# Fetching cached keys page by page through SyncE's queue, and scoring them with four full-height products per sequence

## The chip, the cores and the metric

The kernel runs on one NeuronCore of a Trainium2 chip. The metric is the device time of one execution in microseconds (us), lower being better. Engines are written as in the profile: PE is TensorE (PEld its weight loads), DVE VectorE, ACT ScalarE, POOL GpSimd, SP SyncE, which here issues transfers only. "SPq" is SP's sequencer.

## What is computed

One step of a hybrid decoder layer, for a prompt (512 tokens) and for a sample group (8 sequences of 4 new tokens, with 2048 cached tokens each, kept in pages of 128 tokens). The part that the change touches is the sample group's sparse attention: an indexer scores all cached tokens, the 256 best are chosen, and attention runs over those, here as a mask over all scores.

```python
def dsa_sample(q, k_new, v_new, qi, ki_new, wi, ck, cv, cki, page_table):
    ki_past = cki[page_table].reshape(DB, PAST_LEN, IDX_DIM)   # 16 pages a sequence
    sc = index_scores(qi, wi, ki_all)                          # relu(q.k), weighted sum of 8 heads
    _, idx = lax.top_k(sc, topk)                               # 256 of 2052
    k_sel = ck[phys, off]; v_sel = cv[phys, off]               # 2 kv heads of 64
    return sparse_attend(q, k_sel, v_sel, valid)               # softmax over the chosen
```

Around it stand the input projection (`w_in`), a gated MLP, the prompt's own sparse attention, the memory's key and value projection (`mem_wkv`), the output projection (`w_out`), memory attention (`mem_wq`, `mem_wo`) and, after that, an expert layer that takes most of the time and that the change doesn't touch.

## The kernel before

**The weight stream.** Every projection goes through `wtile` (L219): a tile of weights (128 x 1024, 512 KB) is loaded on SP's queue (L225) into one of two raw buffers, ACT rounds it to a high half (L213), DVE subtracts for the low half (L217), and PE makes 24 products of the three combinations (L249 to L251). Two raw buffers and two of each half mean that the load of a tile waits until the tile two before it has been split. In the order of the program: 19 tiles wA (`w_in`), the memory's normalised input (memT), 8 tiles wKV, then for the first half of the tokens, h0, 8 tiles wO and 4 wMQ, and then the second half, h1, with its own 8 wO.

**Side work.** Between products `tick` lets generators step: the masks' search (L695 on ACT, L692 on DVE), the gated MLP, the prompt's attention (`attend`, L845: softmax L860 to L867, values L880 to L890), and the sample side `samples` (L1251). That is `sample_scores` (index products L1359), `sample_select` (the 256th best score by bisection, 32 bits; one bit is the pass L1413 over 128 x 544 and seven small instructions on DVE, 1412 to 1424), `sample_keys` (key products) and, when both select and keys are done, `sample_attend` (`front` L1531: mask and softmax pieces, `turn`, `values` L1549: 16 products per sequence, L1553, and a copy that frees the buffer). A loop at L469 holds h1 back until `attend` and the sample side have ended, as the sample side's memory is reused there.

**Cached data before.** `index_rows` (L1310) stands behind each of the later weight loads: 4 pairs, so 8 pages of index keys per load on SP's queue, 128 in all (32 KB each, L1319: a register load of the page number, then a DMA with that register in its address). Keys and values come on POOL's queue: `fetch_kv` (L1261) issues four indirect gathers per sequence (L1276) into one of three buffers `kv` (`RING`), and a buffer is fetched anew when its sequence has been used. Two of these three buffers first hold the index keys of sequences 4 to 7. Key scores take 64 products per sequence, each a quarter of the array (64 x 64) by 128 columns (L1496), with weights spread by DVE (`q4`, L1488), and two copies out on ACT (L1500).

Of the kernel before, what the change touches and what calls it, by code (L numbers as in the profile page):

```python
# [18 lines left out]
P = 128  # L19
NP = 512  # L20
NS = 32
# [30 lines left out]
class Kernel:  # L52
# [166 lines left out]
    def wtile(self, pool, src, kt=KT, n=P):  # L219

        more = pool is self.pw and self.gp is not None and self.RX
        if more:
            self.raws = (self.raws + 1) % (2 + self.RX)
        raw = self.t(self.gp, [P, kt, n], tag="wraw", bufs=self.RX) if more and self.raws > 1 else self.t(pool, [P, kt, n], tag="wraw", bufs=2)
        load = self.nc.sync.dma_start(raw, src)  # L225
        self.loads += 1
        if self.todo and self.loads > 2:
            self.index_rows(load)
        hi = self.t(pool, [P, kt, n], F32R, tag="whi", bufs=2)
        lo = self.t(pool, [P, kt, n], F32R, tag="wlo", bufs=2)  # L230
        self.split(hi, lo, raw)
        return hi, lo
# [1046 lines left out]
    def pages(self, s1, s2):  # L1279
        nc, I = self.nc, self.I  # L1280

        pid = self.t(s1, [P, 1])
        for r in range(0, P, 32):
            nc.gpsimd.iota(pid[r : r + 32], [[0, 1]], base=0, channel_multiplier=1, allow_small_or_imprecise_dtypes=True)
        pt_i = self.t(s1, [P, P], I32)
# [3 lines left out]
        self.s_ix = self.t(s1, [P, 64], I32)  # L1289
        tmp = self.t(s1, [P, 64])  # L1290
        for u in range(4):
            r = slice(u * 32, u * 32 + 32)

            nc.vector.tensor_scalar(tmp[r, :32].rearrange("p (b c f) -> p b c f", c=2, f=2),
                                    pf[r].rearrange("p (b c v r f) -> p v r b c f", c=2, v=2, r=2, f=2)[:, u % 2, u // 2],
                                    32.0, pid[r], ALU.mult, ALU.add)
            nc.vector.tensor_scalar(tmp[r, 32:], pf[r].rearrange("p (n u) -> p u n", u=4)[:, u], 32.0, pid[r], ALU.mult, ALU.add)
# [12 lines left out]
    def index_rows(self, behind):  # L1310
        nc = self.nc
        src = self.I["cI"].rearrange("(n d) x -> n d x", d=64)
        with self.tc.issue_after(getattr(behind, "ins", behind)):
            for pt_i, b, m in self.todo[: self.PAGES]:
                for c in range(2):
                    n = b * 16 + 2 * m + c
                    page = nc.values_load(pt_i[:1, n : n + 1], engines=[mybir.EngineType.SP], min_val=0, max_val=src.shape[0] - 1,
                                          skip_runtime_bounds_check_because="a page table holds pages of the pool")
                    nc.sync.dma_start(self.rows[b][c * 64 : c * 64 + 64, m, :], src[bass.ds(page, 1)].rearrange("n d x -> (n d) x"))  # L1319
        self.todo = self.todo[self.PAGES :]  # L1320

    PAGES = 4


    def sample_scores(self, s1, s2):
        nc, I = self.nc, self.I
# [4 lines left out]
        for c in range(2):  # L1331
            src = slice(c * 64, c * 64 + 64)
# [124 lines left out]
    def sample_keys(self, s1, s2):  # L1457
        nc = self.nc
# [9 lines left out]
        self.s_room = Room(qs.rearrange("p e b q -> p (e b q)"))  # L1468
        ps = self.pst("pb")
        for e in range(4):  # L1470
            perm = self.t(s1, [P, P], tag="qst", bufs=2)
            nc.vector.tensor_copy(perm.rearrange("p (u g d) -> p u g d", u=4, g=2),
                                  self.ident.rearrange("p (g e d) -> p e g d", g=2, e=4)[:, e].unsqueeze(1).to_broadcast([P, 4, 2, 16]))
            nc.tensor.matmul(ps[:, e * P : e * P + P], perm, self.s_q.rearrange("p r t -> p (r t)"), start=True, stop=True)
        for e in range(4):
            nc.scalar.activation(qs[:, e].rearrange("p b (r t) -> p r b t", r=4), ps[:, e * P : e * P + P].rearrange("p (r b t) -> p r b t", r=4, b=8),
                                 AF.Copy, scale=0.125)

        own = self.t(s2, [P, 4])
        nc.vector.tensor_reduce(own, self.ident.rearrange("p (r c d) -> p c r d", r=2, d=16), AX.XY, ALU.add)  # L1480
        yield 1.0
        while not self.indexed:
            yield 1.0
        S = [self.t(s1, [P, 4, 512], tag="S8", bufs=2) for _ in range(2)]
        self.s_S = [S[b // 4][:, b % 4, :] for b in range(8)]
        for b in range(8):
            q4 = self.t(s2, [P, 4, 64], tag="q4", bufs=2)
            nc.vector.tensor_tensor(q4.rearrange("p e (c q) -> p e c q", c=4), qs[:, :, b].unsqueeze(2).to_broadcast([P, 4, 4, 16]),  # L1488
                                    own.unsqueeze(1).unsqueeze(3).to_broadcast([P, 4, 4, 16]), ALU.mult)

            pair = [self.pst("pb") for _ in range(2)]
            for e in range(4):
                for f in range(2):
                    for o, ps in zip((0, 64), pair):
                        for c in range(2):
                            nc.tensor.matmul(ps[c * 64 : c * 64 + 64, f * P : f * P + P], q4[o : o + 64, e],  # L1496
                                             self.kv[b][o : o + 64, 2 * c + f, e * P : e * P + P], start=e == 0 and f == 0, stop=e == 3,
                                             skip_group_check=True, tile_position=(o, c * 64))
            for r, ps in enumerate(pair):
                nc.scalar.copy(self.s_S[b].rearrange("p (m r f x) -> p r f m x", m=4, r=2, f=2)[:, r],  # L1500
                               ps[:, : 2 * P].rearrange("p (f m x) -> p f m x", f=2, m=4))
            self.fetch_kv(s2)
            yield 4.0 * self.SK
        self.keyed = True

    SK = 1.0

    def sample_attend(self, s2, s1):
# [40 lines left out]
        def values(b, A):  # L1549
            po = self.pst("pb")  # L1550
            for m in range(4):
                for c in range(4):
                    nc.tensor.matmul(po[c * NS : c * NS + NS, :P], A[:, m, c, :], self.kv[8 + b][:, c, m * P : m * P + P],  # L1553
                                     start=m == 0, stop=m == 3)
            nc.scalar.copy(part(b), po[:, :P])
            self.fetch_kv(s2)
# [314 lines left out]
```

## Time and profile before

| what | value |
|---|---|
| runs shown | 1797.67 us median of 3, 1795.82 to 1801.38 |
| the profiled execution | 1793.41 us, span 1791.7 us |
| mean granted TensorE clock | 0.963 of full speed |
| busy share of the span | PE 94%, DVE 83%, ACT 48%, POOL 28% |
| stage up to the first h1 product | 0 to 403 us |

The span is the time from the first to the last instruction; the execution's own time has 1.7 us beside it. The profiled execution is 4.3 us under the median. A row of a timeline has its start, its length, the engine, the line, what it writes and reads; "[x <-Y]" is the engine's idle time before it and what ended that. A line of the windows has the busy time of each engine in a stretch and the granted clock as a share of full speed.

### The profile page before, as it was taken

What the parts mean: (1) busy time and instruction counts of PE and PEld (TensorE: products, weight loads), DVE (VectorE), ACT (ScalarE), POOL (GpSimd) and SP (SyncE); (2) the same over time, 40 slices, a digit from 0 to 9 for tenths busy, and PEclk for the clock granted to TensorE, in tenths of its full rate; (3) what the DMA queues carried; (4) which work ended last, traced back from release to release, by engine and by line L of the source; (5) the groups of instructions that cost most, each with busy time, mean ns of one, the idle gap of its engine ahead of it and who ended that gap; (6) DMA issues with size and microseconds to landing.
All of it is one profiled execution on the core that took longest, in us unless ns stands there. A gap on an engine that the chain in (4) does not pass through costs nothing. (4 is left out here: it accounts for less than half of the span.)

```text
span 1791.7 us, 30106 instructions
## 1 busy us (share of the span) xinstructions
PE 1675.7 (94%) x10494; PEld 1476.6 (82%) x10494; DVE 1482.9 (83%) x3654; ACT 863.2 (48%) x1584; POOL 503.6 (28%) x437
## 2 busy tenths in 40 slices
PE   7999889989996999799999999999999999999995
PEld 5879757778875889789899998888788888888884
DVE  4586899755759999998999887799898888878897
ACT  4355765764543434674675575233343333333333
POOL 3000123120000054223224222334333534345343
PEclk9999769989998999999999999999999999999997
DMA  5423425445752599789779789799998999999986
GB/s 179 128 83 98 126 85 199 140 166 170 238 172 90 169 345 329 267 316 334 256 269 322 242 306 316 267 353 333 360 356 300 375 357 328 349 334 324 358 305 231
DMA packets 195207, 460.36 MB, mean 257 GB/s; under 512 B 17976, under 2 KB 98616, under 8 KB 193648
## 3 DMA queue, kind: packets, MB, share of 16 engines
q1 hardware_dynamic: 132928, 241.63, 39.7%
q0 software_dynamic: 53072, 207.71, 32.5%
q10 hardware_dynamic: 9056, 9.11, 1.6%
q8 instruction: 82, 1.34, 0.3%
q14 instruction: 69, 0.57, 0.1%
HBM read 416.11 MB, written 42.05 MB: 256 GB/s over the span
## 5 line engine op out<-in xcount | busy, mean ns | idle before, releaser
L251 PE MATMUL t<-t,t 128*128 128x384 f32 (+3 forms) x2544 | 867.9, 346 | 12.5 <-DVE t L217 12.2
L250 PE MATMUL t<-t,t 128*128 128x384 f32 (+3 forms) x2544 | 867.6, 343 | 0.0
L249 PE MATMUL t<-t,t 128*128 128x384 f32 (+3 forms) x2544 | 779.9, 346 | 17.6 <-ACT t L213 15.1
L213 ACT CAST t<-t 128x1024 fp32r<-128x1024 f32 (+4 forms) x512 | 418.2, 841 | 716.8 <-PE t L250 475.8
L217 DVE TENSOR_TENSOR t<-t,t 128x1024 fp32r<-128x1024 f32 (+4 forms) x512 | 488.6, 965 | 140.0 <-ACT t L213 136.3
L251 PEld LDWEIGHTS t<-t,t 128*128 128x128 f32 x2544 | 485.0, 191 | 66.4 <-DVE t L217 15.7
L249 PEld LDWEIGHTS t<-t,t 128*128 128x128 f32 x2544 | 485.0, 191 | 61.2 <-ACT t L213 20.3
L250 PEld LDWEIGHTS t<-t,t 128*128 128x128 f32 x2544 | 485.4, 191 | 38.4 <-issue 5.7
L1276 POOL DMA_INDIRECT t<-in_u,t x160 | 201.7, 1260 | 499.0 <-DVE t L1736 305.0
L1276 POOL DMA_INDIRECT t<-in_v,t x160 | 215.5, 1347 | 298.0 <-DVE t L1741 233.9
L1741 DVE SCALAR_TENSOR_TENSOR t<-t,t,t 128x1024 f32<-128x1024 f32 x160 | 204.9, 1281 | 4.5 <-DMA t<-in_v,t 3.6
L1736 DVE SCALAR_TENSOR_TENSOR t<-t,t 128x1024 f32<-128x1024 f32 x160 | 193.8, 1219 | 8.7 <-DMA t<-in_u,t 8.6
L1081 ACT ACTIVATE t<-t 128x512 f32<-128x512 f32 x96 | 96.6, 1148 | 19.3 <-DMA wd<-t 18.5
L1276 POOL DMA_INDIRECT t<-in_cK,t x32 | 32.3, 1009 | 212.1 <-PE t L1359 146.5
L1217 DVE TENSOR_TENSOR t<-t,t 128x352 f32<-128x352 f32 x128 | 66.6, 521 | 6.2 <-DMA t<-wd 4.0
L1097 ACT ACTIVATE t<-t 128x384 f32<-128x384 f32 x128 | 62.3, 487 | 11.8 <-PE t L251 9.2
L1071 ACT ACTIVATE t<-t,t 128x128 f16<-128x128 f16 x192 | 58.2, 395 | 10.1 <-DVE t L1067 7.4
L1078 PE MATMUL t<-t,t 128*128 128x128 f16 x384 | 51.8, 221 | 9.4 <-ACT t L1081 8.8
L1276 POOL DMA_INDIRECT t<-in_cV,t x32 | 34.2, 1069 | 72.0 <-PE t L1553 45.1
L695 ACT ACTIVATE t<-t,t 128x384 f32<-128x384 f32 x64 | 42.7, 666 | 24.4 <-DVE t L692 20.3
L1079 PE MATMUL t<-t,t 128*128 128x128 f16 x384 | 49.7, 221 | 0.4 <-DVE t L1073 0.3
L1079 PEld LDWEIGHTS <-t 128*128 128x128 f16 x384 | 36.7, 98 | 10.6 <-issue 10.1
(400 smaller groups left out, 1471.2 us busy)
## 6 DMA issues: line engine op xcount, KB each, us to landing
t<-in_uT SPq DMA_DIRECT2D x128, 512.0 KB, 5.8
t<-in_v SPq DMA_DIRECT2D x128, 512.0 KB, 6.2
wd<-t POOLq DMA_DIRECT2D x11, 2048.0 KB, 9.2
t<-wd SPq DMA_DIRECT2D x32, 704.0 KB, 7.9
gd<-t SPq DMA_DIRECT2D x56, 192.0 KB, 5.3
t<-gd SPq DMA_DIRECT2D x56, 192.0 KB, 7.6
t<-in_wA SPq DMA_DIRECT2D x19, 512.0 KB, 4.0
t<-in_wO SPq DMA_DIRECT2D x16, 512.0 KB, 4.0
```

The lines of the kernel that those rows point to most:

```text
L213: self.nc.scalar.copy(hi, x)
L217: self.pin_v = self.nc.vector.tensor_tensor(lo, x, hi, ALU.subtract)
L249: mm(out, ah, bh, start=first, stop=False)
L250: mm(out, ah, bl, start=False, stop=False)
L251: self.pin = mm(out, al, bh, start=False, stop=last)
L1079: nc.tensor.matmul(o, oj[:, x, :], ol[:, x, :], start=False, stop=True)
L1081: nc.scalar.activation(wb[:, :, t : t + 4].rearrange("p i t -> p t i"), ps.rearrange("p (t i) -> p t i", t=4), AF.Copy, scale=1.0 / 2048.0)
L1097: nc.scalar.activation(G, ps, AF.Gelu_apprx_tanh)
L1217: nc.vector.tensor_tensor(q(w)[:, : 4 * NB - 1], self.wp[:, :, i % 4, :], q(G)[:, : 4 * NB - 1], ALU.mult)
L1276: self.nc.gpsimd.indirect_dma_start(out=out, out_offset=None, in_=src, in_offset=bass.IndirectOffsetOnAxis(ap=ix, axis=0))
L1736: nc.vector.scalar_tensor_tensor(r, r, 1.0, hf, ALU.mult, ALU.mult, accum_out=a[:, k : k + 1])
L1741: nc.vector.scalar_tensor_tensor(acc, r, a[:, k : k + 1], acc, ALU.mult, ALU.add)
```

## The change

Index pages and key pages form one list, `todo`, of (target, source, place in the page table). Behind every weight load after the second, `fetch_pages` issues the next 6 of it on SP's queue: first the 128 index pages, then 128 key pages (64 KB each, 128 x 128). Key pages of a sequence enter the list when its buffer is taken. `sample_keys`, before it scores a sequence, calls `fetch_pages` until that sequence's 16 pages have been issued, with a pause worth 4 us of ticks between the calls. Values are gathered as before. Key scores become four products per sequence, 128 x 32 by 512 columns, side by side in one PSUM bank, with one copy out. Lines below L1260 shift: page load L1281, index product L1357, key product L1485, copy L1487, a bit's pass L1411, `front`'s first softmax piece L1524, value products L1540, the last products of the sample side L1621 and L1622 (before L1634, L1635).

```diff
@@ wtile
-        load = self.nc.sync.dma_start(raw, src)
+        self.pin_s = self.nc.sync.dma_start(raw, src)
         self.loads += 1
-        if self.todo and self.loads > 2:
-            self.index_rows(load)
+        if self.loads > 2:
+            self.fetch_pages()
@@ fetch_kv
             kv = self.t(s2, [P, 2048], tag="kv", bufs=self.RING)
-            kv = kv.rearrange("p (m x) -> p m x", m=4)
-            for m in range(4):
-                self.gather(kv[:, m, :], self.I["cV" if n >= 8 else "cK"], self.s_ix[:, n * 4 + m : n * 4 + m + 1])
+            if n < 8:
+                src = self.I["cK"].rearrange("(n d) (e x) -> n e d x", d=32, e=4)
+                self.todo += [(kv[:, m * P : m * P + P], src, 16 * n + m) for m in range(16)]
+            else:
+                for m in range(4):
+                    self.gather(kv[:, m * 512 : m * 512 + 512], self.I["cV"], self.s_ix[:, (n - 8) * 4 + m : (n - 8) * 4 + m + 1])
...
+    def fetch_pages(self):
+        nc = self.nc
+        with self.tc.issue_after(getattr(self.pin_s, "ins", self.pin_s)):
+            for out, src, n in self.todo[: self.PAGES]:
+                page = nc.values_load(self.s_pt[:1, n : n + 1], engines=[mybir.EngineType.SP], min_val=0, max_val=src.shape[0] - 1,
...
+                x = src[bass.ds(page, 1)]
+                nc.sync.dma_start(out, x.rearrange("n d x -> (n d) x") if len(x.shape) == 3 else x[0])
+        self.todo = self.todo[self.PAGES :]
+
+    PAGES = 6
@@ pages (index_rows, with PAGES = 4 pairs, is gone; the gathers' indices shrink from 64 to 32 columns)
-        self.todo, self.loads = [(pt_i, b, m) for b in range(8) for m in range(8)], 0
+        src = I["cI"].rearrange("(n d) x -> n d x", d=64)
+        self.todo, self.loads = [(self.rows[b][c * 64 : c * 64 + 64, m, :], src, 16 * b + 2 * m + c) for b in range(8) for m in range(8) for c in range(2)], 0
@@ sample_scores
-            while any(x[1] == b for x in self.todo):
+            while len(self.todo) > 16 * (7 - b + len(self.kv)):
                 yield 1.0
@@ sample_keys
-        qs = self.t(s2, [P, 4, 8, 16])
...
+        perm = self.t(s1, [P, P], tag="qst", bufs=2)
+        nc.vector.tensor_copy(perm.rearrange("p (e g d) -> p e g d", e=4, g=2), self.ident.rearrange("p (g e d) -> p e g d", g=2, e=4))
         ps = self.pst("pb")
...
+        nc.tensor.matmul(ps[:, :256], perm, qb.rearrange("p b g r t -> p (b g r t)"), start=True, stop=True)
+        room = self.t(s2, [P, 512])
+        q3 = room[:, :256].rearrange("p (b q) -> p b q", b=8)
+        nc.scalar.copy(room[:, :256], ps[:, :256])
...
         for b in range(8):
-            q4 = self.t(s2, [P, 4, 64], tag="q4", bufs=2)
...
-            pair = [self.pst("pb") for _ in range(2)]
-            for e in range(4):
-                for f in range(2):
-                    for o, ps in zip((0, 64), pair):
-                        for c in range(2):
-                            nc.tensor.matmul(ps[c * 64 : c * 64 + 64, f * P : f * P + P], q4[o : o + 64, e],
...
-            for r, ps in enumerate(pair):
-                nc.scalar.copy(self.s_S[b].rearrange("p (m r f x) -> p r f m x", m=4, r=2, f=2)[:, r],
...
+            while len(self.todo) > 16 * (min(len(self.kv), 8) - b - 1):
+                self.fetch_pages()
+                yield self.SP
+            ps = self.pst("pb")
+            for c in range(4):
+                nc.tensor.matmul(ps[c * NS : c * NS + NS, :], q3[:, b], self.kv[b][:, c * 512 : c * 512 + 512],
+                                 start=True, stop=True)
+            nc.scalar.copy(self.s_S[b].rearrange("p (m u x) -> p u m x", m=4, u=4), ps.rearrange("p (u m x) -> p u m x", u=4, m=4))
             self.fetch_kv(s2)
             yield 4.0 * self.SK
         self.keyed = True
 
+    SP = 4.0
     SK = 1.0
```

**Where the order moves.** SP, from the fourth-last wKV tile on (t_3695 is its load; `in_wKV` and `in_wO` are weights, `in_cK` key pages; a page is a register load, an address step "ISA" and the DMA). Before:

```order
L225 DMA t_3695<-in_wKV 128x1024
L225 DMA t_3788<-in_wKV 128x1024
L225 DMA t_3878<-in_wKV 128x1024
L225 DMA t_3971<-in_wKV 128x1024
L225 DMA t_4083<-in_wO 128x1024
```

The same queue in the changed kernel, from the last wKV load (t_3472) to the first wO load (t_3656):

```order
L225 DMA t_3472<-in_wKV 128x1024
L1278 TENSOR_LOAD t_123
L1281 ISA
L1281 DMA t_2383<-in_cK 128x1x128
...
L1278 TENSOR_LOAD t_123
L1281 ISA
L1281 DMA t_2383<-in_cK 128x1x128
L225 DMA t_3656<-in_wO 128x1024
```

Ten pages now stand between these two loads. From behind the fifth wKV load to the fourth wMQ load of h0 there are 126 pages (2 of index keys, 124 of keys) and 15 loads; before there was none there.

PE, at the end of h0's last wMQ tile. Before, the products of that tile (t_5032, L249 to L251) alternate with the sample side's softmax (L1535) and values (L1553):

```order
L1553 MATMUL t_4748<-t_4474,t_4733 32x128 x16
L249 MATMUL t_5032<-t_152,t_5028 128x256
...
L1545 MATMUL t_4772<-t_60,t_2890 128x128 x4
L1535 LDWEIGHTS t_4779
L1535 MATMUL t_4778<-t_2676,t_4779 128x512
L250 MATMUL t_5032<-t_153,t_5028 128x256
...
L251 MATMUL t_5032<-t_152,t_5029 128x256
L778 MATMUL t_5114<-t_150,t_4870 128x256 x2
L1553 MATMUL t_4786<-t_4593,t_4771 32x128 x16
```

In the changed kernel the tile (t_4928) ends first, then the last key product stands (L1485), and behind it all of `sample_attend`, from the first softmax product (L1522) to the eighth value product, with h1's first product (t_5487) after it:

```order
L251 MATMUL t_4928<-t_144,t_4925 128x256
L1485 MATMUL t_4953<-t_4344,t_2598 32x512
...
L1522 LDWEIGHTS t_5004
L1522 MATMUL t_5003<-t_3527,t_5004 128x512
...
L1540 MATMUL t_5050<-t_4604,t_5015 32x128 x16
...
L1540 MATMUL t_5363<-t_5285,t_5356 32x128 x13
...
L1622 MATMUL t_5419<-t_2598,t_762 128x32 x4
L249 MATMUL t_5487<-t_5439,t_5483 128x288
```

Before, four of the eight value products (L1553) stand among projections; now none does.

DVE, around the split of the last wMQ tile (t_4906 is the raw tile; L1411 is a bit's pass) and the first of h1's wO tiles (t_5481):

```order
L1411 SCALAR_TENSOR_TENSOR t_3531,t_3548<-t_3530,t_3546,t_58 128x544
L1412 STREAM_TRANSPOSE t_3549<-t_3548 128x32
L1413 TENSOR_REDUCE t_3550<-t_3549 128x8
L217 TENSOR_TENSOR t_4925<-t_4906,t_4924 128x1024
...
L1411 SCALAR_TENSOR_TENSOR t_3531,t_3548<-t_3530,t_3546,t_58 128x544
...
L217 TENSOR_TENSOR t_5484<-t_5481,t_5483 128x1024
```

26 of the 32 bits stand in the changed order before the last wMQ split and 6 behind it; before the change all 32 stand before the split of the third wO tile.

## Rows read from the trace of the kernel before

**Rows 1.** Windows: us, busy of PE, PEld, DVE, ACT, POOL, then PEclk, DMA share, GB/s

```profile
210.00:251.00 41.00, 26.51 (x223) 18.61 (x222) 33.48 (x200) 31.20 (x96) 11.73 (x12) 0.54 0.27 78
251.00:308.00 57.00, 54.02 (x605) 44.32 (x605) 54.24 (x224) 32.35 (x77) 20.25 (x20) 0.97 0.50 162
...
371.00:403.00 32.00, 26.13 (x236) 20.41 (x235) 17.94 (x72) 17.82 (x54) 6.78 (x7) 0.84 0.45 157
```

**Rows 2.** PE timeline: start us, us, engine line op [idle before <-releaser]

```profile
221.07 5.45 PE L1496 MATMUL t<-t,t 64*64 64x128 f32 x64 [5.96 <-ACT t L1500]
...
251.19 0.58 PE L249 MATMUL t<-t,t 128*128 128x256 f32 x1
```

**Rows 3.** PE groups: count | busy us, mean ns | idle before

```profile
L1496 PE MATMUL t<-t,t 64*64 64x128 f32 x512 | 27.3, 322 | 9.6 <-ACT t L1500 9.6
...
L1672 PE MATMUL t<-t,t 128*32 128x256 f32 x64 | 4.5, 387 | 0.0
```

**Rows 4.** SP timeline, DMA issues: start us, us, what, how many

```profile
42.98 0.53 SPq L225 DMA_DIRECT2D t<-in_wA  x1
44.02 7.35 SPq L1319 DMA_DIRECT2D t<-in_cI  x8
...
144.51 24.20 SPq L1319 DMA_DIRECT2D t<-in_cI  x24
...
258.17 25.32 SPq L225 DMA_DIRECT2D t<-in_wKV  x4
...
333.03 15.49 SPq L225 DMA_DIRECT2D t<-in_wMQ  x4
```

**Rows 5.** One line's instructions on SP, L225: duration ns min/median/max

```profile
L225 SPq DMA_DIRECT2D t<-in_wKV x8: 327/328/382, 178.7 to 283.2; - x8
```

**Rows 6.** DMA issues: KB each, median us from issue to landing

```profile
t<-in_wA SPq DMA_DIRECT2D x19, 512.0 KB, 4.0
...
t<-in_cI SPq DMA_DIRECT2D x128, 32.0 KB, 2.0
```

**Rows 7.** ACT groups from 208 to 252

```profile
L695 ACT ACTIVATE t<-t,t 128x512 f32<-128x512 f32 (+1 forms) x25 | 16.7, 667 | 7.0 <-DVE t L692 6.8
L695 ACT ACTIVATION_READ_ACCUMULATOR t<-t,t 128x1 f32 x25 | 4.7, 187 | 0.0
```

**Rows 8.** ACT timeline: last squares of the memory, and the third wKV tile's split

```profile
207.88 0.42 ACT L132 ACTIVATE t<-t 128x256 f32<-128x256 f32 x1 [0.34 <-PE t L135]
...
255.75 1.05 ACT L213 CAST t<-t 128x1024 fp32r<-128x1024 f32 x1 [1.78 <-PE t L250]
```

**Rows 9.** DVE timeline: three bits' passes, then the first softmax piece of the attention

```profile
305.62 0.79 DVE L1413 SCALAR_TENSOR_TENSOR t<-t,t,t 128x544 f32<-128x544 f32 x1
...
307.98 0.79 DVE L1413 SCALAR_TENSOR_TENSOR t<-t,t,t 128x544 f32<-128x544 f32 x1
...
312.46 0.78 DVE L1413 SCALAR_TENSOR_TENSOR t<-t,t,t 128x544 f32<-128x544 f32 x1
...
333.70 0.69 DVE L1537 CUSTOM_DVE_ANT_0 t<-t,t 128x512 f32<-128x512 f32 x1
```

**Rows 10.** DVE groups of the page: the split of a weight tile

```profile
L217 DVE TENSOR_TENSOR t<-t,t 128x1024 fp32r<-128x1024 f32 (+4 forms) x512 | 488.6, 965 | 140.0 <-ACT t L213 136.3
```

**Rows 11.** PE timeline: last wMQ product, values of sequences 4 and 7, first h1 product

```profile
370.79 0.28 PE L251 MATMUL t<-t,t 128*128 128x256 f32 x1
...
371.86 1.08 PE L1553 MATMUL t<-t,t 128*32 128x128 f32 x32
...
384.39 1.08 PE L1553 MATMUL t<-t,t 128*32 128x128 f32 x32 [0.73 <-ACT t L1546]
...
403.10 0.48 PE L249 MATMUL t<-t,t 128*128 128x288 f32 x1
```

**Rows 12.** POOL timeline: gathers of one sequence's values

```profile
374.92 0.95 POOL L1276 DMA_INDIRECT t<-in_cV,t  x1 [0.30 <-PE t L880]
376.17 0.95 POOL L1276 DMA_INDIRECT t<-in_cV,t  x1 [0.30 <-issue]
```

More of the change, by code (lines that the diff above doesn't have):

```diff
@@ L1264, in fetch_kv @@
             kv = self.t(s2, [P, 2048], tag="kv", bufs=self.RING)
-            kv = kv.rearrange("p (m x) -> p m x", m=4)
-            for m in range(4):
-                self.gather(kv[:, m, :], self.I["cV" if n >= 8 else "cK"], self.s_ix[:, n * 4 + m : n * 4 + m + 1])
-            self.kv.append(kv)
+            if n < 8:
[4 more added lines that the diff above has]
+                    self.gather(kv[:, m * 512 : m * 512 + 512], self.I["cV"], self.s_ix[:, (n - 8) * 4 + m : (n - 8) * 4 + m + 1])
+            self.kv.append(kv)
+    def fetch_pages(self):
[3 more added lines that the diff above has]
+                page = nc.values_load(self.s_pt[:1, n : n + 1], engines=[mybir.EngineType.SP], min_val=0, max_val=src.shape[0] - 1,
+                                      skip_runtime_bounds_check_because="a page table holds pages of the pool")
+                x = src[bass.ds(page, 1)]
+                nc.sync.dma_start(out, x.rearrange("n d x -> (n d) x") if len(x.shape) == 3 else x[0])
+        self.todo = self.todo[self.PAGES :]
+    PAGES = 6
     RING = 3
@@ L1284, in pages @@
             nc.gpsimd.iota(pid[r : r + 32], [[0, 1]], base=0, channel_multiplier=1, allow_small_or_imprecise_dtypes=True)
-        pt_i = self.t(s1, [P, P], I32)
+        pt_i = self.s_pt = self.t(s1, [P, P], I32)
         nc.gpsimd.dma_start(pt_i, I["page_table"].rearrange("b n -> (b n)").partition_broadcast(P))
@@ L1288, in pages @@
         nc.vector.tensor_copy(pf, pt_i)
-        self.s_ix = self.t(s1, [P, 64], I32)
-        tmp = self.t(s1, [P, 64])
+        self.s_ix = self.t(s1, [P, 32], I32)
+        tmp = self.t(s1, [P, 32])
         for u in range(4):
             r = slice(u * 32, u * 32 + 32)
[L1294 to L1297, printed above, removed]
+            nc.vector.tensor_scalar(tmp[r], pf[r].rearrange("p (n u) -> p u n", u=4)[:, u], 32.0, pid[r], ALU.mult, ALU.add)
         nc.vector.tensor_copy(self.s_ix, tmp)
@@ L1304, in pages @@
             self.rows.append(kx[:, b % 2 * 2 : b % 2 * 2 + 2, :].rearrange("p b (m x) -> p (b m) x", x=P))
-        self.todo, self.loads = [(pt_i, b, m) for b in range(8) for m in range(8)], 0
+        src = I["cI"].rearrange("(n d) x -> n d x", d=64)
+        self.todo, self.loads = [(self.rows[b][c * 64 : c * 64 + 64, m, :], src, 16 * b + 2 * m + c) for b in range(8) for m in range(8) for c in range(2)], 0
         for _ in range(self.RING - 2):
             self.fetch_kv(s2)
[L1310 to L1314, printed above, removed]
-                for c in range(2):
[L1316 to L1322, printed above, removed]
     def sample_scores(self, s1, s2):
@@ L1465, in sample_keys @@
                 nc.vector.tensor_scalar(qb[r, :, g, q], self.s_q[r, q].rearrange("p (b t) -> p b t", t=4), 0.125, None, ALU.mult)
-        qs = self.t(s2, [P, 4, 8, 16])
-        self.s_room = Room(qs.rearrange("p e b q -> p (e b q)"))
+        perm = self.t(s1, [P, P], tag="qst", bufs=2)
+        nc.vector.tensor_copy(perm.rearrange("p (e g d) -> p e g d", e=4, g=2), self.ident.rearrange("p (g e d) -> p e g d", g=2, e=4))
         ps = self.pst("pb")
-        for e in range(4):
[L1471 to L1480, printed above, removed]
+        nc.tensor.matmul(ps[:, :256], perm, qb.rearrange("p b g r t -> p (b g r t)"), start=True, stop=True)
+        room = self.t(s2, [P, 512])
+        q3 = room[:, :256].rearrange("p (b q) -> p b q", b=8)
+        nc.scalar.copy(room[:, :256], ps[:, :256])
+        self.s_room = Room(room)
         yield 1.0
@@ L1486, in sample_keys @@
         for b in range(8):
-            q4 = self.t(s2, [P, 4, 64], tag="q4", bufs=2)
-            nc.vector.tensor_tensor(q4.rearrange("p e (c q) -> p e c q", c=4), qs[:, :, b].unsqueeze(2).to_broadcast([P, 4, 4, 16]),
-                                    own.unsqueeze(1).unsqueeze(3).to_broadcast([P, 4, 4, 16]), ALU.mult)
-            pair = [self.pst("pb") for _ in range(2)]
-            for e in range(4):
-                for f in range(2):
-                    for o, ps in zip((0, 64), pair):
-                        for c in range(2):
-                            nc.tensor.matmul(ps[c * 64 : c * 64 + 64, f * P : f * P + P], q4[o : o + 64, e],
-                                             self.kv[b][o : o + 64, 2 * c + f, e * P : e * P + P], start=e == 0 and f == 0, stop=e == 3,
-                                             skip_group_check=True, tile_position=(o, c * 64))
-            for r, ps in enumerate(pair):
-                nc.scalar.copy(self.s_S[b].rearrange("p (m r f x) -> p r f m x", m=4, r=2, f=2)[:, r],
-                               ps[:, : 2 * P].rearrange("p (f m x) -> p f m x", f=2, m=4))
+            while len(self.todo) > 16 * (min(len(self.kv), 8) - b - 1):
[6 more added lines that the diff above has]
+            nc.scalar.copy(self.s_S[b].rearrange("p (m u x) -> p u m x", m=4, u=4), ps.rearrange("p (u m x) -> p u m x", u=4, m=4))
             self.fetch_kv(s2)
```

2 lines of the change are left out of this document (1 added, 1 removed).

## The prediction, made before the changed kernel had run

> **What bounds the kernel now.** I read the page first: PE is busy 94% of the span, so only a stretch where PE idles or runs at its lower clock has something to give, and any stretch left bare of projections costs in full. Then the windows up to h1's first product, where the two programs differ; behind it they are the same but for small reorderings, so whatever that product shifts by, the end shifts by. Two stretches stand out. From 210 to 251 PE is busy 26.51 of 41.00 us at a granted clock of 0.54, and from 371 to 403 it is busy 26.13 of 32.00 at 0.84; between, from 251 to 308, it is busy 54.02 of 57.00 at 0.97 [rows 1]. A granted clock near 0.5 is the 1.2 GHz level, near 1 the 2.4 GHz level. The PE timeline shows the first stretch to be the block of key products, which wait up to 5.96 us for the ACT copies; the first wKV product comes at 251.19 [rows 2]. In the second stretch the projections have run out: the last wMQ product starts at 370.79, values of four sequences follow, and h1's first product starts at 403.10, when the sample side has ended [rows 11]. So the end is set by when the sample side ends: select on DVE, softmax, values. The SP view tells what paces the weights: in the wKV, wO and wMQ stages SP issues weight loads alone, held back by buffers, not by its own work [rows 4].
>
> **What the change removes.** 512 quarter products cost 27.3 us of PE and 9.6 us of idle before them. Four side by side with 256 columns cost 4.5 us for 64 products, so 0.28 us for four; at 512 columns I take double, 0.56, times 8 sequences: 4.5 us [rows 3]. With the 9.6 us gone too, the gain on PE would be 27.3 + 9.6 - 4.5 = 32 us if nothing else bound. The copies and spread queries that go on ACT and DVE lie beside other work; the 32 gathers of keys leave POOL, which isn't waited for there; both cost and give nothing by themselves.
>
> **Where that moves the start of wKV.** Two things. First, 24 index pages in one go held SP for 24.20 us behind the 17th wA load [rows 4]; with 6 pages behind each load the 18th goes out 18 x 0.95 = 17 us earlier. PE could use some of that only, as it was working on two loaded tiles; I take 8 us (bounds 0 and 17), so the memory's last squares come at 200 instead of 207.88 [rows 8]. Second, from those squares to the third wKV tile's split ACT took 47.9 us [rows 8]. In the changed order it has 9 passes of the masks' search there instead of 25; 16 fewer, at (16.7 + 4.7 + 7.0) / 25 = 1.14 us with their waits [rows 7], is 18 us, and six copies and the waits for the key block are another 3 to 6. That leaves 26: the split at 226, and the load behind it, which came 2.4 us after the split (258.17 against 255.75) [rows 4, 8], at about 229. First wKV product at about 222. At this point the changed kernel is 29 us ahead. I count it as 220 to 242 for the load of the fifth wKV tile.
>
> **What it adds: SP's queue.** From that load to the load of h0's fourth wMQ tile, SP issues 126 pages and 15 weight loads in the program's order, where before it issued weight loads alone. A page costs SP 7.35 / 8 = 0.92 us in a run behind a load and 24.20 / 24 = 1.01 in the long run; a load to the page behind it is 44.02 - 42.98 = 1.04 [rows 4]. I take 0.95: 126 x 0.95 + 15 x 1.04 = 135 us. The key pages are 64 KB where the rows are of 32 KB; a weight load of 512 KB costs SP 0.33 us [rows 5], so bytes are not what SP pays for; the register in the address is. So the load of the last wMQ tile goes out at 229 + 135 = 364, against at most 348.5 before (333.03 + 15.49) [rows 4]. Landing takes 4.0 us [rows 6], the two splits 2 to 3 on ACT and DVE, 0.97 of it DVE's [rows 10]: split at about 371. While SP paces, loads are 7 to 12 us apart and PE, with 3 us of products a tile, waits on each; the 29 us of lead are gone.
>
> Here the Trainium skill ("DMA: Bandwidth & Descriptors", section "Issuing engines are not separate DMA queues") speaks another way: it says that the time a sequencer needs to start a DMA is usually small next to the transfer. The trace disagrees for these pages: about 1.0 us of SP for each [rows 4], with 2.0 us to landing [rows 6], half of it. By the rule pages would not pace anything; the sum for that is the first rival.
>
> **What it does to select.** The bits of select are on DVE between the weight splits, and an engine works in order: a split that waits for a late tile holds the bits behind it. One bit takes 307.98 - 305.62 = 2.36 us undisturbed [rows 9]. In the changed order 26 bits stand before the last wMQ split and 6 behind it. So front(0), which was at 333.70 [rows 9], comes after the split at 371 by: 6 x 2.36 = 14 us of bits; two splits of h1 tiles, 2; some twenty memory-softmax instructions between, about 5; the end of select, which lay with other work in 333.70 - 312.46 = 21.2 us before [rows 9], and of which I take 10 as its own with its waits (bounds 7 and 21); about 3 of waits for PE. Front(0) at 405.
>
> **What it does to the tail.** Before, four of eight sequences' values lay among the wMQ products. Now all eight stand bare behind the last one. The value gathers' ring holds three; five more sequences must wait for a buffer, and each costs POOL four gathers of 376.17 - 374.92 = 1.25 us, 5.0 [rows 12]. Five times 5.0 and about 4 to land after the last is 29 us behind the first values at 410 (front to values I estimate as 5): the eighth at about 439. The last four sequences before were done in 384.39 - 371.86 = 12.5 us [rows 11], 4.2 each, with their gathers already ahead, so 29 for eight is no outlier. From the last values to h1's first product it took 403.10 - 384.39 = 18.7 us [rows 11], which had eight memory-softmax groups of PE in it that are now earlier; I take 13 (bounds 9 and 19). h1's first product at 452.
>
> **Sum.** 452 - 403 = 49 us later. Profiled 1793.4 + 49 = 1842; that execution is 4.3 us below the median of the runs shown, so the median is 1797.7 + 49 = **1847 us**. A change in pages by 0.05 us each is 6 us; the bounds of start (+13, -9), tail (+6, -4) and end of select (+11, -3) are 15 to 20 us either way together: 1830 to 1868 for this case.
>
> **Rivals.**
> 1. *Pages cost SP little, DVE paces* (0.17). If a page costs as a weight load does, 0.33 [rows 5], SP needs 126 x 0.33 + 15.6 = 57 us. Then the stage is held by DVE, which needs for 26 bits 61 us, for 15 splits 15 [rows 9, 10] and for softmax and masks an estimated 30: about 110 us, and the last wMQ split comes at 340 to 348 instead of 371. The tail is the same: 23 to 31 us less, about 1820 (1812 to 1830). Against it stand two rows of pages at 0.92 and 1.01.
> 2. *Slower still* (0.13). A key page has 128 pieces of 512 B where an index page has 64, and none is in the trace; if one costs 0.3 us more, 124 x 0.3 = 37 us: 1884. It also holds that PE between late tiles falls to the 1.2 GHz level as it did at 0.54 from 210 to 251 [rows 1]; 3 us of products a tile become 5, which are under the 7 us between loads, so that alone adds nothing until wMQ. Against it: a weight load, with 128 rows too, costs 0.33 [rows 5].
> 3. *Not slower* (0.10). The 32 us of PE and the earlier start outweigh the tail. It needs front(0) no later than 403 - 47 = 356, the 47 being the same tail; so the last wMQ split at 322. That decides at a page price of (322 - 7 - 229 - 15.6) / 126 = 0.56 us, with DVE's 110 us of work shrunk by a sixth. Or the values run at 4.2 us each with gathers ahead, which moves the bound by some 8 us. It would give 1785 to 1800.
>
> **How the numbers follow.** Forecast 0.60, rivals 0.17, 0.13 and 0.10. Of the third, 0.07 is faster by over 0.3% (5.4 us, about what a measurement of this kernel can tell from no change) and 0.03 within it; the rest within it, 0.02, is taken from the low edge of the first rival. Faster 0.07, same 0.05, slower 0.88. The range reaches from the first rival's low edge, 1812, to the slower case's near side, 1880: it leaves out most of rival 3 and half of rival 2, under 0.2.
>
> **What the profile after would show.** SP: pages and loads in unbroken runs from about 229 to 364, 0.95 us a page, loads 7 us and more apart. PE: first wKV product at about 222; key products (L1485) 4 to 5 us in all; waits for DVE and ACT splits (L217, L213) ahead of most wO and wMQ tiles, with a granted clock near 0.5 to 0.8; no product of L249 to L251 from about 377 to 452. DVE: bits of L1411 up to about 390, L1524 first at 405. Values (L1540) eight times, 3.5 to 5 us apart. Wrong would be: SP idle in that stretch (rival 1), a page over 1.2 us (rival 2), a last wMQ split before 325 (rival 3), or a stage behind h1's first product that is longer than before by more than 5 us, which no step here accounts for.

## The result, and the profile after

| kernel | median of the runs | ratio to before |
|---|---|---|
| before | 1797.6 us | |
| changed | 1904.2 us (1900.5 to 1910.6, 4 runs) | 1.0594, 95% interval 1.0559 to 1.0629 |

The changed kernel is 106.5 us slower; I had forecast 49 slower, and the range ended at 1880. The profiled execution has a span of 1904.4 us, 112.7 over that of before. The windows of the changed kernel up to h1's first product (columns as in [rows 1]):

```profile
276.00:386.00 110.00, 77.74 (x402) 48.21 (x402) 53.46 (x208) 40.62 (x82) 4.95 (x4) 0.82 0.31 94
386.00:425.00 39.00, 20.92 (x80) 11.61 (x76) 18.66 (x67) 4.20 (x5) 4.22 (x4) 0.76 0.36 108
425.00:464.00 39.00, 16.06 (x78) 11.43 (x77) 31.00 (x118) 8.50 (x19) 4.19 (x4) 0.72 0.32 104
464.00:518.00 54.00, 36.21 (x369) 28.49 (x372) 18.16 (x83) 20.67 (x63) 19.83 (x24) 0.76 0.46 143
```

PE, which was busy for 54.02 of 57 us in the wKV stage before [rows 1], is now busy for 77.74 of 110, 20.92 of 39 and 16.06 of 39, at granted clocks of 0.72 to 0.82. The PE timeline of the changed kernel gives the places that answer to [rows 2, 11]:

```profile
212.17 0.58 PE L249 MATMUL t<-t,t 128*128 128x256 f32 x1
...
272.05 1.07 PE L1485 MATMUL t<-t,t 128*32 128x512 f32 x8
...
435.86 1.04 PE L1485 MATMUL t<-t,t 128*32 128x512 f32 x2
...
462.19 0.21 PE L1549 MATMUL t<-t,t 128*128 128x32 bf16 x1 [19.30 <-DVE t L1451]
...
468.41 1.69 PE L1540 MATMUL t<-t,t 128*32 128x128 f32 x32
...
513.44 0.85 PE L249 MATMUL t<-t,t 128*128 128x288 f32 x2 [0.64 <-ACT t L213]
```

The first wKV product comes at 212.17, 39 us earlier than before (251.19), and h1's first product at 513.44, 110.3 us later than before (403.10). So 110.3 of the 112.7 us of span arise ahead of that product, and all the 39 us gained at the start are lost on the way. SP, the same view as [rows 4]:

```profile
221.96 0.34 SPq L225 DMA_DIRECT2D t<-in_wKV  x1
...
225.15 15.00 SPq L1281 DMA_DIRECT2D t<-in_cK  x10
...
240.25 0.38 SPq L225 DMA_DIRECT2D t<-in_wKV  x1
...
241.32 8.39 SPq L1281 DMA_DIRECT2D t<-in_cK  x6
...
358.14 27.76 SPq L1281 DMA_DIRECT2D t<-in_cK  x18
...
425.02 0.38 SPq L225 DMA_DIRECT2D t<-in_wMQ  x1
```

From the fifth wKV load (221.96) to the last wMQ load (425.02) SP takes 203.1 us, and issues in unbroken runs. A key page costs it 8.39 / 6 = 1.40 to 27.76 / 18 = 1.54 us by the run, 1.47 on the mean of the 124, not 0.92 to 1.01 as the index pages of before [rows 4]. The line's instructions on SP (duration min/median/max) show a part of that in the DMA instruction itself:

```profile
L1281 SPq DMA_DIRECT2D t<-in_cI x128: 468/469/1279, 17.8 to 224.2; - x128
...
L1281 SPq DMA_DIRECT2D t<-in_cK x128: 558/591/662, 225.1 to 430.8; - x128
```

Who waits for SP is seen in PE's waits between 222 and 425 (us in total, times, longest):

```profile
PE t L1485 <- DMA t<-in_cK: 25.3, 8, 6.3
PE t L854 <- DVE t L860: 20.0, 1, 20.0
...
PE t L249 <- ACT t L213: 5.0, 4, 1.8
```

It is the key products that wait for key pages, 25.3 us in 8 waits, and the projections that follow them in PE's order are held up with them; the splits of the late tiles, where I had expected the waits, cost 5 us. The 20.0 us for the prompt's softmax (L860) are no wait for SP: with no key pages on SP (below) there is a wait of 16.8 us at the same place. That softmax comes behind the masks' search, whose last pass on ACT starts at 248.1, and before the change at 244.6. DVE at the end of the stage (split of the last wMQ tile, the last bit, front's first softmax piece), then all 32 bits' passes (first and last start), as against 206.1 to 312.5 before, whose line stands last:

```profile
431.78 1.22 DVE L217 TENSOR_TENSOR t<-t,t 128x1024 fp32r<-128x1024 f32 x1
...
453.14 0.79 DVE L1411 SCALAR_TENSOR_TENSOR t<-t,t,t 128x544 f32<-128x544 f32 x1
...
463.79 0.69 DVE L1524 CUSTOM_DVE_ANT_0 t<-t,t 128x512 f32<-128x512 f32 x1
```

```profile
L1411 DVE SCALAR_TENSOR_TENSOR t<-t,t,t x32: 764/785/787, 295.1 to 453.1; 128x544 f32<-128x544 f32 x32
```

```profile
L1413 DVE SCALAR_TENSOR_TENSOR t<-t,t,t x32: 776/785/787, 206.1 to 312.5; 128x544 f32<-128x544 f32 x32
```

### The profile page after: what moved, and what is told of

Its sections match the earlier page's. It is cut to its first block, busy times and chain, and to the rows that moved or that the text cites. A ratio compares the mean times of both kernels' runs of the same rounds, so it can differ in the third digit from the quotient of the medians.

```text
span 1904.4 us, 29723 instructions
## 1 busy us (share of the span) xinstructions
PE 1697.6 (89%) x10038; PEld 1466.0 (77%) x10040; DVE 1488.2 (78%) x3638; ACT 861.9 (45%) x1573; POOL 464.5 (24%) x405
## 5 line engine op out<-in xcount | busy, mean ns | idle before, releaser
L251 PE MATMUL t<-t,t 128*128 128x384 f32 (+3 forms) x2544 | 871.2, 347 | 21.0 <-DVE t L217 20.7
L249 PE MATMUL t<-t,t 128*128 128x384 f32 (+3 forms) x2544 | 781.7, 347 | 17.7 <-ACT t L213 15.9
L213 ACT CAST t<-t 128x1024 fp32r<-128x1024 f32 (+5 forms) x512 | 418.6, 842 | 761.8 <-PE t L250 460.7
L217 DVE TENSOR_TENSOR t<-t,t 128x1024 fp32r<-128x1024 f32 (+5 forms) x512 | 487.5, 963 | 189.6 <-ACT t L213 167.6
L251 PEld LDWEIGHTS t<-t,t 128*128 128x128 f32 x2544 | 487.8, 192 | 77.4 <-DVE t L217 27.9
L249 PEld LDWEIGHTS t<-t,t 128*128 128x128 f32 x2544 | 487.6, 192 | 71.8 <-ACT t L213 24.6
L1485 PE MATMUL t<-t,t 128*32 128x512 f32 x64 | 29.4, 783 | 25.3 <-DMA t<-in_cK 25.3
```

What stands on the lines that cost most here:

```text
L213: self.nc.scalar.copy(hi, x)
L217: self.pin_v = self.nc.vector.tensor_tensor(lo, x, hi, ALU.subtract)
L249: mm(out, ah, bh, start=first, stop=False)
L251: self.pin = mm(out, al, bh, start=False, stop=last)
```

## The experiments

The names: SP is the theory that page issues on SP pace the stage; L that the select starts late and ends the stage. "Ratio" is to the kernel before, with its 95% interval; a time without a ratio is that of one run.

### What a key page costs SP

Key pages read as they lie, with the queries permuted to fit:

```diff
-                src = self.I["cK"].rearrange("(n d) (e x) -> n e d x", d=32, e=4)
+                src = self.I["cK"].rearrange("(n d) (e x) -> n (d e) x", d=32, e=4)
-        nc.vector.tensor_copy(perm.rearrange("p (e g d) -> p e g d", e=4, g=2), self.ident.rearrange("p (g e d) -> p e g d", g=2, e=4))
+        nc.vector.tensor_copy(perm.rearrange("p (g d e) -> p g d e", g=2, e=4), self.ident.rearrange("p (g e d) -> p g d e", g=2, e=4))
```

> The key pages are read as they lie (128 rows of 512 B, one after the other), and the permutation of the queries is changed to fit; everything else as in the changed kernel, the result the same. Theory A, a key page costs SP more than an index page because of its reordered address pattern: SP's run of ten pages falls from 15.0 to about 9.5 us (0.95 a page), and with 126 pages on the path the time falls by about 60 us, to 1840 to 1850. Rivals B and C, it is the number of 512 B pieces (128 against 64) or the bytes (64 KB against 32): a page stays at 1.4 to 1.5 us and the time at 1895 to 1910.

Measured: 1860.3 us, one run. SP's rows in this kernel:

```profile
224.26 8.06 SPq L1281 DMA_DIRECT2D t<-in_cK  x10
...
312.91 15.01 SPq L1281 DMA_DIRECT2D t<-in_cK  x18
...
350.85 0.38 SPq L225 DMA_DIRECT2D t<-in_wMQ  x1
```

A page costs 8.06 / 10 = 0.81 and 15.01 / 18 = 0.83 us in these two runs of pages, 0.82 on the mean of the 124 (0.75 to 0.97 by the run), for the same 64 KB in the same 128 pieces of 512 B. The last wMQ load goes out at 350.85, 74 us earlier than in the changed kernel. Theory A holds for what sets the price; the price itself is under the 0.95 that it gave. The time fell by 44 and not by 60 us, since something else then ends the stage:

```profile
405.89 0.21 PE L1549 MATMUL t<-t,t 128*128 128x32 bf16 x1 [33.24 <-DVE t L1451]
```

PE has no work left and waits 33.24 us for L1451, the end of select.

The same bytes in half as many pieces:

```diff
+                src = self.I["cK"].rearrange("(n d) (e x) -> n (d e) x", d=32, e=2)
-                self.todo += [(kv[:, m * P : m * P + P], src, 16 * n + m) for m in range(16)]
+                self.todo += [(kv[m % 2 * 64 : m % 2 * 64 + 64, m // 2 * 256 : m // 2 * 256 + 256], src, 16 * n + m) for m in range(16)]
```

> Each key page is read as 64 pieces of 1 KB into half of the partitions: same bytes, half the pieces, as an index page has. The keys lie wrongly in the buffer for it, so the key scores are of other numbers. Theory B, SP pays by the piece: a page costs about 0.95 us as an index page does, and the time falls to 1840 to 1850. Theory C, SP pays by the byte: a page stays at 1.4 to 1.5 us, 1895 to 1910. Theory A (pattern) expects 0.95 here too, and is told apart by the other run.

Measured: 1850.1 us, one run.

```profile
225.26 9.46 SPq L1281 DMA_DIRECT2D t<-in_cK  x10
...
320.28 18.82 SPq L1281 DMA_DIRECT2D t<-in_cK  x18
```

0.95 to 1.05 us a page in these two, 0.95 on the mean (0.88 to 1.05): more than with 128 pieces. So a page does not get cheaper with fewer pieces, and the reordered pattern alone takes it from 0.82 to 1.47 at equal pieces and bytes. The DMA instruction by itself (duration min/median/max) shows the same order, first as it lies, then in 64 pieces; with the reordered pattern its median was 591, and for an index page, of half the bytes in 64 pieces, 469:

```profile
L1281 SPq DMA_DIRECT2D t<-in_cK x128: 3/333/1554, 224.3 to 354.2; - x128
```

```profile
L1281 SPq DMA_DIRECT2D t<-in_cK x128: 3/468/1022, 225.3 to 368.7; - x128
```

The 64 pieces also go to 64 partitions and not to 128; these two are not told apart. That this run is 10 us faster than the one with cheaper pages is one run against one, and nothing is read from it.

### SP's part of the loss

No key pages on SP:

```diff
-                self.todo += [(kv[:, m * P : m * P + P], src, 16 * n + m) for m in range(16)]
+                whole = self.I["cK"].rearrange("(n d) (e x) -> (d e) n x", d=32, e=4)[:, 16 * n : 16 * n + 16]
+                self.todo += [(kv.rearrange("p (m x) -> p m x", m=16), whole, -1)] + [(None, None, -1)] * 15
```

> The 128 key pages are left out of SP's queue; one DMA per sequence with a fixed address fetches 16 pages in the order in which they lie (not by the page table, so other keys are scored). All else, the program's order too, as in the changed kernel. Theory SP (the page issues on SP pace the stretch from the fifth wKV load to the last wMQ split): loads come as buffers free, the stretch falls from 203 us to about 100 to 120, what is left is DVE's work, and h1's first product comes at 410 to 430 instead of 513: 1800 to 1825. Rival, the stage is long because of its bytes, of the split order on DVE or of the key products, and not because of SP: h1's first product after 480, over 1870. Bare tail: it stays at 75 to 85 us from the last wMQ split to h1's first product in either case.

Measured: 1846.5 us, ratio 1.0269 (1.0241 to 1.0296), 0.0325 of 1797.6 or 58 us less than the changed kernel. From the fifth wKV load to the last wMQ load, the stretch that took 203.1 us, it is now at most 326.40 - 221.71 = 104.7, within the 100 to 120 that theory SP expected:

```profile
221.71 0.33 SPq L225 DMA_DIRECT2D t<-in_wKV  x1
...
308.82 17.58 SPq L225 DMA_DIRECT2D t<-in_wMQ  x4
```

But h1's first product comes at 449.69, not at 410 to 430, and 1846 is over the expected time; a second cost stands behind the first. PE's row at the end of the stage, and the bits:

```profile
398.70 0.18 PE L1553 MATMUL t<-t,t 128*128 128x32 bf16 x1 [41.43 <-DVE t L1455]
```

```profile
L1415 DVE SCALAR_TENSOR_TENSOR t<-t,t,t x32: 774/785/787, 280.4 to 389.7; 128x544 f32<-128x544 f32 x32
```

PE waits 41.43 us for the end of select, whose first bit starts at 280.4, where before it was 206.1. From the last wMQ split, at 333.56 at the latest, to h1's first product it is 116 us, not the expected 75 to 85: the end of select sets it.

### The late select

One number of the kernel before, 8 pages per load made 6:

```diff
-    PAGES = 4
+    PAGES = 3
```

> The kernel before with one number changed: 6 index pages behind each weight load, not 8; keys gathered and scored as before. Theory L (late select): the index keys are complete only with the 24th load instead of the 18th, the last index product and with it the first of 32 bits come 50 to 80 us later than 206, and since 32 bits and the end of select need over 110 us of DVE, front(0) comes after the wMQ stage: 1825 to 1850. Rival, the step of the prediction by which pages spread more thinly free the wA stage and nothing else: 1785 to 1797.

Measured: 1860.0 us, ratio 1.0333 (1.0302 to 1.0364), 60 us slower by the ratio and over the expected 1850, with keys gathered and scored as before. Index products of the kernel before, then of this one, its bits (first and last start), and PE at the end of the stage:

```profile
L1359 PE MATMUL t<-t,t x128: 217/275/323, 117.3 to 194.5; 128*128 128x64 f32 x128
```

```profile
L1359 PE MATMUL t<-t,t x128: 217/275/323, 118.3 to 270.4; 128*128 128x64 f32 x128
```

```profile
L1413 DVE SCALAR_TENSOR_TENSOR t<-t,t,t x32: 765/785/805, 295.5 to 395.6; 128x544 f32<-128x544 f32 x32
```

```profile
404.68 0.18 PE L1562 MATMUL t<-t,t 128*128 128x32 bf16 x1 [22.93 <-DVE t L1453]
```

The last index product moves from 194.5 to 270.4, the first bit from 206.1 to 295.5, and PE then waits 22.93 us for select. The rival, my own step that thinner pages only free the wA stage, falls. The wait is a part of the 60 us; the whole is what the one number costs.

The changed kernel with 8 per load, then with both costs cut, in two ways (each `PAGES = 6` made `8`, on the kernels above):

> The changed kernel with 8 pages behind each load, not 6; all else as changed. Theory SP and L together: index keys are in by the 18th load, first bit at 205 to 225; key pages begin with the 19th load at about 177 and cost 128 x 1.47 + 25 loads = 215 us of SP, so the last wMQ load goes out at about 390 and h1's first product comes at 440 to 460: 1830 to 1855. SP alone (select doesn't matter): the sum of SP's work is the same as before this edit, so 1890 to 1905.

Measured: 1872.9 us, ratio 1.0420 (1.0386 to 1.0453): 31 us less than with 6, but over the expected 1830 to 1855. A run of 16 pages holds SP for 24 us, and here the weights of wKV wait behind it:

```profile
221.73 24.22 SPq L1281 DMA_DIRECT2D t<-in_cK  x16
```

> 8 pages behind each load, and the key pages left out of SP's queue (one DMA of a fixed address per sequence, so other keys are scored). Theory SP and L: 1780 to 1800, h1's first product at 390 to 405. If select's start doesn't matter: 1840 to 1848, as with 6.

Measured: 1801.8 us, ratio 1.0014 (0.9997 to 1.0030). With no key pages on SP and the index keys as early as before, the loss is gone:

```profile
L1415 DVE SCALAR_TENSOR_TENSOR t<-t,t,t x32: 767/785/787, 201.4 to 318.4; 128x544 f32<-128x544 f32 x32
```

So, taken away in this order, 0.0594 falls apart as 0.0325 (SP's key pages), 0.0255 (6 pages per load instead of 8) and 0.0014: 58, 46 and 3 us. The shares hang on the order, as the two costs overlap: with 8 per load first (1.0420) it is 31 us for the pages per load and then 73 for SP's key pages. In either order each of them costs, and together they make up the loss.

With both gone the change is worth nothing all the same. The first wKV product comes at 218.43 in this kernel, 33 us earlier than before, h1's first product at 400.92, only 2 earlier; between them PE waits once for 25.4 us for the prompt's softmax (L854 on L860), a wait that the kernel before doesn't have. The masks' search, which that softmax follows, ends no earlier than before. That this wait eats the lead is read from the trace; no run took it away.

To see whether the 46 us are indeed the select's end, the search was cut short in the kernel with 6 per load and fixed addresses:

```diff
-        for bit in range(31, -1, -1):
+        for bit in range(31, 15, -1):
```

> 6 pages behind each load and no key pages on SP, as in the run with fixed addresses that took 1846 us; and the search for the 256th best score stops after 16 of 32 bits (so more than 256 are kept, and other keys are scored). Theory L (the stage ends when the late select ends): 16 bits of 2.3 us are gone from the end, front(0) at about 363 instead of 400, and the time falls by 35 to 40 us, to 1806 to 1814. Rival, the thinner index pages cost their 45 us elsewhere (in the wA, memory or wKV stage, or in the bare values): the time stays within 10 us of 1846.

Measured: 1799.5 us, ratio 1.0029 (1.0015 to 1.0042), 47 us less than with 32 bits, more than the expected 35 to 40.

```profile
L1415 DVE SCALAR_TENSOR_TENSOR t<-t,t,t x16: 774/785/786, 280.9 to 346.9; 128x544 f32<-128x544 f32 x16
```

```profile
360.11 0.19 PE L1553 MATMUL t<-t,t 128*128 128x32 bf16 x1 [7.12 <-DVE t L1455]
```

The bits end at 346.9 and not at 389.7, and PE's wait for select shrinks from 41.43 to 7.12 us. Theory L is borne out: the bits stand at the end of the stage. The same cut in the kernel before, where the bits have slack, was not run, so how much of the 47 us is merely work taken off DVE stays open.

### Looking for a version that beats both

Key pages on SP as they lie, 8 per load:

> Both costs cut: contiguous key pages (0.84 us each) and 8 pages behind each load; the result is the same. Theory SP and L: key pages cost SP 128 x 0.84 = 108 us from about 177 on, the last wMQ load goes out at 315 to 335, select is done at about 330 to 345; h1's first product at 395 to 415: 1785 to 1810, so about as fast as before. If a third cost is behind the changed kernel's time (the order of the tail, the products): over 1825.

Measured: 1826.4 us, ratio 1.0151 (1.0118 to 1.0185), a miss by 16 us.

```profile
294.81 14.30 SPq L1281 DMA_DIRECT2D t<-in_cK  x16
...
312.35 13.36 SPq L1281 DMA_DIRECT2D t<-in_cK  x16
```

Runs of 16 pages hold the wO loads for 13 to 14 us each. The condition set above for a third cost, over 1825, is met. It is neither the order of the tail nor the products: the kernel with fixed addresses and 8 per load has both the same and differs only in how the keys are fetched, and it is at 1.0014. So 0.0137, 25 us, is what key pages on SP still cost at the lower price.

Key pages on POOL's queue (16 of a sequence when its buffer comes free, read as they lie), first with 6 index pages per load, then 8:

```diff
-                self.todo += [(kv[:, m * P : m * P + P], src, 16 * n + m) for m in range(16)]
+                for m in range(16):
...
+                    self.nc.gpsimd.dma_start(kv[:, m * P : m * P + P], src[bass.ds(page, 1)].rearrange("n d x -> (n d) x"))
```

> Key pages are issued by POOL, all 16 of a sequence when its buffer comes free; index pages stay on SP, 6 behind a load; result the same. Theory SP: SP's queue is free of the 188 us of key pages, loads come as buffers free. A page on POOL I estimate at 1.0 to 1.6 us (the gathers take 0.95 and 0.30 between), so 16 to 26 us a sequence behind a ring of three: the eighth sequence's keys are in at about 222 + 8 x 20 = 380, so the last wMQ tile's products, behind which the last key product stands, are not much later, and h1's first product comes at 430 to 470: 1820 to 1860. Rival (not SP): over 1880.

Measured: 1861.8 us, ratio 1.0348 (1.0320 to 1.0376), 44 us less than the changed kernel and just over the expected range: the same pages, by the page table, but not on SP. A page costs POOL 265.78 - 264.85 = 0.93 us, and no weight load stands in that queue:

```profile
264.85 0.54 POOL L1271 DMA_DIRECT2D t<-in_cK  x1 [207.41 <-PE t L1361]
265.78 0.54 POOL L1271 DMA_DIRECT2D t<-in_cK  x1 [0.40 <-issue]
```

> Key pages (contiguous) issued by POOL when a buffer comes free, and 8 index pages behind each load on SP, as before; the four products of the changed kernel; result the same. Theory SP and L: with both costs taken away, first bit at 200 to 210 as before; POOL's pages (0.94 us each) of sequences 1 and 2 are in by 225, later ones follow at 15 us a sequence while wKV and wO run; h1's first product at 395 to 410: 1785 to 1805, equal to before within 0.5%, and below it by up to 10 us if the standstill for key copies was worth something. If the wide products or the pages have a cost of their own: over 1815.

Measured: 1825.4 us, ratio 1.0134 (1.0111 to 1.0158), again a miss by 20 us. PE's longer waits in this kernel:

```profile
217.63 0.28 PE L1398 MATMUL t<-t,t 32*128 32x32 f32 x1 [9.33 <-DVE t L1392]
...
272.90 1.65 PE L854 MATMUL t<-t,t 64*128 64x384 f32 x2 [9.37 <-DVE t L860]
...
359.67 0.21 PE L1550 MATMUL t<-t,t 128*128 128x32 bf16 x1 [15.87 <-DVE t L1455]
```

The first waits for select's first copy on DVE (L1392), and the first bit starts at 219 with it, the second for the prompt's softmax (L860), the third for the end of select. The second by itself doesn't make a kernel slower than before: the kernel with fixed addresses and 8 per load, as fast as before, has it too, and longer:

```profile
PE t L854 <- DVE t L860: 25.9, 2, 25.4
```

Two tries with the bits placed earlier among the products (`COUNT = 1.2` made `0.9`), on that kernel and, as the control, on the kernel before:

> The kernel with keys on POOL and 8 index pages behind each load, and one number more: a bit of select counts 0.9 us of the side work's clock, not 1.2, so the bits stand earlier among the projections and the softmax and value products of the sample side among more of the wMQ tiles. What is left there over the kernel before, 28 us, I put down to the order of the bits on DVE against the prompt's softmax and the splits (PE waits of 9.4, 15.9 us for it). Theory order: 5 to 20 us come back, 1805 to 1820. Rival, the key pages themselves (waits for in_cK on PE, 5.7 us): unchanged within 4 us, 1821 to 1829.

> The kernel before with the same number, 0.9 for 1.2, as the control. In it select already ends under the wO tiles (last bit 312 of 371), so the bits have slack: 1793 to 1805, no difference that can be measured; earlier bits could cost where they stand ahead of a split (up to 10 us more).

Measured: 1820.7 us, ratio 1.0145 (1.0116 to 1.0175), no difference from 1.0134; and 1803.6 us, ratio 1.0054 (1.0029 to 1.0079), a little slower than before. The first try moved the bits little (last one at 343.1, not 350.6) and PE's wait for the end of select was 19.3 us, not shorter than 15.87, so it says nothing of what a select that ends earlier would bring. No version beat the kernel before. The two that fetch keys by the page table and cut both costs stay 24 to 27 us over it: with the pages on SP that is what these still cost there, with the pages on POOL it was not settled. The waits above name places, but no run took one of them away. Nor does it all lie ahead of h1: in the kernel with pages on SP as they lie and 8 per load, h1's first product is 15 us later than before and the rest of the span 18 us longer.

## Why the prediction was wrong

**What held.** The direction, and the chain: SP's queue from the fifth wKV load to the last wMQ load, then split, six bits, the end of select, front, eight bare values, h1. The steps outside SP came out near: first wKV product 212 (forecast 222), fifth wKV load 222 (229), last load to split 6.8 us (7), split to front(0) 463.79 - 431.78 = 32 us (34), front(0) to h1 513.44 - 463.79 = 49.7 us (47). The last is in part luck: from the first values to the eighth (L1540, 468.41 to 503.87) it took 35 us and not 29, and from there to h1 10 and not 13.

**The term that was mis-sized** is "I take 0.95" for a key page. The stretch took 203.1 us, not 135: 68 us more, of which 124 key pages at a mean of 1.47 make 124 x 0.52 = 64. With the 7 us earlier start that is the miss of 61 us at h1's first product. I reasoned that bytes don't matter since a 512 KB load costs 0.33. The runs don't show them to matter either, but the index pages that I took the price from are read as they lie, and the reordered pattern of a key page is what the price hangs on. My rival for it had 0.3 us as its step and the piece count as its reason; the runs show 0.5 and the pattern.

**A second step failed under the first.** I carried the late select as a passenger of SP: bits behind late splits. It is a bound of its own. With pages cheaper than I assumed (0.81 to 0.83), the time was 1860, not under 1847; with none on SP, where my first rival gave 1820, it was 1846. The thinner index pages did free the start (the lead at the first wKV product was 39 us, forecast 29), but they cost 31 to 60 us further on, by the kernel they are tried in, a term that the sum didn't have: six instead of eight pages behind a load delay the last index key from the 18th load to the 24th, behind the memory stage, and 32 bits at 2.36 us and more have nothing to hide under when they start at 280 to 295. The row was there: before, the bits took 206 to 312, and front(0) came at 333.70 [rows 9], so a start 75 us later had to end at about 408, whatever SP did.

**The rule that I weighed** (the Trainium skill, "DMA: Bandwidth & Descriptors", "Issuing engines are not separate DMA queues", that a sequencer's time to start a DMA is usually small next to the transfer) would have given my first rival. The trace was right to be preferred: 58 us of the loss, and 73 in the other order, are the issuing queue's.

**The products.** I forecast 4.5 us for all key products, and misread the row: each of these fp32 products leaves two records in the trace. By the program the 64 records of L1672 are 32 products, and the 512 of L1496 are 256, 32 for a sequence and not 64 as I wrote. So four products of 256 columns take 0.56 us and not 0.28, and the whole is 9.0 and not 4.5; the time that I forecast doesn't go by this term. The group in the page is

```profile
L1485 PE MATMUL t<-t,t 128*32 128x512 f32 x64 | 29.4, 783 | 25.3 <-DMA t<-in_cK 25.3
```

The first sequence's four products, whose pages had all landed, took 1.07 us together (272.05, eight records), as the corrected sum says. Many later ones start when their own pages land and run alone for about as long: 1.04 us for two records at 435.86. A lower granted clock adds to it: two records at 330.20 took 1.88 us, at a granted clock of 0.50 against 1.00 at 435.86. With fixed addresses and 6 per load, where the products of a sequence start together, the same group was busy for 9.3 us:

```profile
L1489 PE MATMUL t<-t,t 128*32 128x512 f32 x64 | 9.3, 603 | 0.6 <-DMA t<-in_cK 0.6
```

## What to carry to other kernels

When transfers are spread more thinly to relieve a queue, follow the last of them, not the mean: its consumer (here a serial search on DVE) may be the longest chain of the stage. Price an issue on a queue by a row with the same address pattern, and multiply it by all that stands in that queue before the next urgent load. When a forecast has one bound, work out at what time the next chain would end if that bound were free: here it was 58 us of the one and then 46 of the other, 73 and 31 the other way round.

## What the runs showed of the hardware

SP's price for a DMA with a register in its address, register load included, at 64 KB: 1.47 us on the mean with a reordered source pattern, 0.82 with the same 128 pieces of 512 B as they lie, 0.95 as 64 pieces of 1 KB (one run); an index page of 32 KB in 64 pieces cost 0.92 and 1.01 in the rows of before. Fewer and larger pieces on 64 partitions were not cheaper than 128 on all partitions. POOL issued the pages, as they lie, at 0.93 us each.
